# Operand splits and the last gate rank placed later in the queues, and the down projection's summed products accumulated in one PSUM bank

## The chip, the cores and the metric

The kernel runs on one core of a Trainium2 chip. The metric is device time in microseconds (us), the median of the runs of one program. The engines are PE (TensorE), DVE (VectorE), ACT (ScalarE), POOL (GpSimd) and SP (SyncE, which here only issues DMAs).

## What is computed

One hybrid decoder layer on a 1024 x 1024 activation in float32: two attention groups, an output projection, and a gated feed-forward part with a causal convolution of width 3. Only the feed-forward part is touched by the change:

```python
h = rmsnorm(x, ffn_norm_g[l])
u = causal_dwconv(h @ w_up[l], conv_w[l], conv_b[l])
gate, val = jnp.split(u, 2, axis=-1)
x = x + (jax.nn.silu(gate) * val) @ w_down[l]
```

`w_up` is 1024 x 5632 (2816 gate and 2816 value columns), `w_down` is 2816 x 1024.

## The kernel before

**Precision.** Each float32 factor is split into a high part (a cast on ACT) and a low part (source minus high part, on DVE or POOL). `mm3` makes one product block from three matmuls: high x high, high x low, low x high. A **split** below is the cast and the subtraction; lines 762 and 763 split an activation operand, lines 908 and 910 a weight.

**Seven products instead of eight.** The feed-forward matrices are multiplied as 2 x 2 blocks with seven products by the scheme of Strassen and Winograd. `PORD` names them: a11, s2, a22, a12, s1, s3, s4. Each has an activation operand (`bmat`: b11, t2, t4, b21, t1, t3, b22 in that order) and a weight block (raw, or one of four sums that POOL makes on lines 881 to 890). One product is 4 x 3 matmuls of 128 x 512, or 3 x 3 in the last two chunks.

**Steps.** There are 34 steps of seven products. Steps 0 to 21 are the up projection; each leaves one rank of 128 gate and 128 value rows, which DVE combines, convolves (`conv`, line 1007, four long instructions a rank), and gates (line 1083 on ACT, line 1084 on DVE). Steps 22 to 33 are the down projection in three chunks `c` of the inner dimension (`KN` = 4, 3, 3 block pairs), four steps each. The last two ranks (20 and 21) go through a plain product at the end.

**Where one operand set gives way to the next.** Activation operands wait in DRAM (`td`). In the last step of the up projection, and in the last step of a chunk, each product is followed by `operands(n, ...)`: SP loads that product's next operand blocks into seven buffers `st`, ACT and DVE split them (the first block of each is split on POOL) into the tiles that PE has just read for the last time. There are three such handovers: step 21 to 22, 25 to 26 and 29 to 30.

**The y tiles.** In the down projection DVE adds each product from its PSUM bank into the output tiles `y` in SBUF. These tiles take the memory of the up projection's pool `upp`, which holds the convolution's tiles, so their first load (line 1102) can only run when the last of those is done with. Each product has a bank of its own; eight banks go round.

**What sets the order.** SP's instructions keep the order in which the program is written. For the other engines a list scheduler decides by priority, which is the place in the program unless `tc.high_priority(offset=...)` shifts it; each engine then runs its own list strictly in order. Weights are made at most four products ahead (`ahead_to(idx + 4)`) into three pair buffers `wspl`. Weight splits of step 22 stand on POOL and DVE, later ones all on DVE.

Of the kernel before, what the change touches and what calls it, by code (L numbers as in the profile page):

```python
# [9 lines left out]
F32 = mybir.dt.float32  # L10
F32R = mybir.dt.float32r
BF16 = mybir.dt.bfloat16
AF = mybir.ActivationFunctionType
ALU = mybir.AluOpType
# [3 lines left out]
P = 128  # L18
# [7 lines left out]
NJ = DFF // P  # L26
NPRE = 3
# [19 lines left out]


PORD = ("a11", "s2", "a22", "a12", "s1", "s3", "s4")
LO_UP = ("s3", "s1")  # L50
LO_FIRST = ("a11", "a22", "a12")

ORDER, ORDER_LAST = (0, 1, 3, 2), (0, 1, 3, 2)
LAG, LEAD, RATE, PAUSE, TRC = 3, 40.0, 1.327, 12.0, 0.67
UA = 3

PARTS = ((0, 512), (512, 256), (768, 256))
NORM_AT = ((1, 3), (2, 3), (3, 0))
# [10 lines left out]
def layer(ctx, tc, xT, wqk, wv0, wv, wout, wup, wdn, cols, fbias, yT):  # L69
    nc = tc.nc  # L70
    act = nc.scalar.activation
# [84 lines left out]
                    if d == 1:  # L156
                        n.split(min(n.pieces, int(frac * n.pieces + 0.01)))

    def mm3(ps, ah, al, bh, bl, start, stop):
        nc.tensor.matmul(ps, ah, bh, start=start, stop=False)  # L160
        nc.tensor.matmul(ps, ah, bl, start=False, stop=False)  # L161
        nc.tensor.matmul(ps, al, bh, start=False, stop=stop)  # L162

    small = ctx.enter_context(tc.tile_pool(name="small", bufs=4))

# [168 lines left out]
    with tc.tile_pool(name="ps_0", bufs=6, space=PSUM) as ps0, \  # L334
# [31 lines left out]
        for k in range(KT):  # L366
# [4 lines left out]
            for u in range(2):  # L371
                wh, wl = w_qk[u].get()
                for c in range(2):
                    if k == 0:
                        psq[u, c] = ps0.tile([P, 512], F32, name="p0")
                    sl = slice(c * 512, (c + 1) * 512)
# [363 lines left out]
    def bank():  # L740
        turn[0] += 1
        if (turn[0] - 1) % 8 < 6:
            return ps_u.tile([P, 512], F32, name="u")
        return ps_p.tile([P, 512], F32, name="pj")
# [27 lines left out]
    for c in range(2):  # L772
        sl = slice(c * 512, (c + 1) * 512)
        for m in range(KT):
# [8 lines left out]
            if c == 0 and m < 2:  # L783
                ps = box[m]
            else:
                ps = bank()
                for k in range(4):
                    w, _ = out_step(1 + c, m, c, k, ps)
# [27 lines left out]
    tp_ = ctx.enter_context(tc.tile_pool(name="tblk", bufs=1, side="right"))  # L816
    t2, t4, t1, t3, b22 = (halves(tp_, n) for n in ("t2", "t4", "t1", "t3", "b22"))

    def product(w, o, b, n=4):
        ps = bank()  # L820
        wh, wl = w
        for k in range(n):
            sl = slice(o + k * P, o + (k + 1) * P)
            mm3(ps, wh[:, sl], wl[:, sl], b[k][0], b[k][1], k == 0, k == n - 1)
        return ps

    steps = [("u", j, 4) for j in range(NJ)] + [(c, mp, KN[c]) for c in range(NCH) for mp in range(KT // 2)]
    NS = len(steps)
# [17 lines left out]
    first(1)  # L846
    first(2)

    stream = [(j, n) for j in range(NS) for n in PORD if j >= NPRE or n not in ("a11", "a12")]
    made, tiles, plain = {}, {}, {}  # L850
    pos = [0]

# [150 lines left out]
    def conv(t, u, us):  # L1003
        cw = C_CW + 3 * u
        act(t, us, AF.Identity, scale=col[:, cw + 2:cw + 3], bias=gcol(C_CB, u))
        for s, tap in ((1, 1), (2, 0)):
            nc.vector.scalar_tensor_tensor(t[:, s:], us[:, :T - s], col[:, cw + tap:cw + tap + 1],  # L1007
                                           t[:, s:], op0=ALU.mult, op1=ALU.add)
# [5 lines left out]
    def operand(dst, src, eng=None):  # L1014
        raw = stp.tile([P, 512], F32, name="st")
        nc.sync.dma_start(raw, src)
        split(dst, raw, eng)

    def operands(n, c):
        for i in range(KN[c]):  # L1020
# [24 lines left out]
    for j in range(NJ):  # L1045
# [31 lines left out]
            if j == NJ - 1:  # L1077
                operands(n, 0)
        tv = upp.tile([P, T], F32, name="tv")
        conv(tv, 2 * j + 1, ub)  # L1080
        tg = stg.tile([P, T], F32, name="tg", tag="hl")
        conv(tg, 2 * j, ua[j])
        act(tg, tg, AF.Silu)
        tt(tg, tg, tv, ALU.mult)
        if j % 2 == 0:
            prev = tg
        elif j < PLAIN:
# [23 lines left out]
    for s in range(NJ, NS):  # L1111
        c, mp, kn = steps[s]
        ev, od_ = 2 * mp, 2 * mp + 1
        for n in PORD:
            ahead_to(idx + 4)
            if s == NS - 1 and n == PORD[3]:
                plain_split(0)
            if s == NS - 1 and n == PORD[-1]:
                plain_split(1)
            w, o = made[s, n]  # L1120
            idx += 1
            ps = product(w, o, bmat[n], kn)
            if c == 0 and n == PORD[0]:
                if mp == 0:
                    load_y(0)
                elif mp < KT // 2 - 1:
                    load_y(mp + 1)
            if c == 0 and mp == 0 and n == PORD[3]:
                load_y(1)
            if n == "a11":  # L1130
                m1s = fin.tile([P, 512], F32, name="m1s")
                nc.scalar.copy(m1s, ps)
                tt(y[ev, 0], y[ev, 0], m1s, ALU.add)
            elif n == "s2":
                u2 = fin.tile([P, 512], F32, name="u2")
                tt(u2, ps, m1s, ALU.add)
                tt(y[ev, 1], y[ev, 1], u2, ALU.add)
            elif n == "a22":
                tt(y[od_, 0], y[od_, 0], ps, ALU.subtract)
            elif n == "a12":  # L1140
                tt(y[ev, 0], ps, y[ev, 0], ALU.add)
            elif n == "s1":
                tt(y[od_, 1], ps, y[od_, 1], ALU.add)
                tt(y[ev, 1], ps, y[ev, 1], ALU.add)
            elif n == "s3":
                tt(u2, ps, u2, ALU.add)
                tt(y[od_, 1], y[od_, 1], u2, ALU.add)
                tt(y[od_, 0], y[od_, 0], u2, ALU.add)
            elif n == "s4":
                tt(y[ev, 1], ps, y[ev, 1], ALU.add)  # L1150
            if mp == KT // 2 - 1 and c < NCH - 1:
                operands(n, c + 1)
            if c == 1 and mp == 1 and kind[n] < 4:
                i = kind[n]
                rest[i // 2, i % 2] = spare[i]
                operand(spare[i], td[-1][i])
# [124 lines left out]
```

## Time and profile before

| | us |
|---|---|
| median of 3 runs (lowest to highest) | 1423.91 (1421.47 to 1424.47) |
| the profiled execution | 1431.94 |
| its span, first to last instruction | 1430.2 |
| PE busy in the span | 1310.7 (92%) |
| DVE busy | 1111.7 (78%) |
| POOL busy | 773.8 (54%) |
| ACT busy | 620.7 (43%) |

The profiled execution is 8.0 us longer than the median. Times inside the trace count from the start of its span. The up projection's last step runs from about 1148 to 1168, the down projection from there to 1391, and the plain product and the final norm fill the rest. Busy PE time is modelled; counts of matmuls in a stretch, and the gaps between their starts, are the surer reading.

### The profile page before, as it was taken

To read this page: it belongs to the slowest core of one execution; us is meant where nothing else is said; L and a number is where in the kernel's file an instruction comes from. 1 tells how busy PE (TensorE), PEld (TensorE's weight loads), DVE (VectorE), ACT (ScalarE), POOL (GpSimd) and SP (SyncE) were. 2 spreads that over 40 slices of the span, in tenths; PEclk is the share of its full clock that TensorE was granted. 3 is DMA by queue.
4 is the path that set the end of the run, shared out by engine and by line. 5 is a ranking of instruction groups with operands and counts; after the bars stand their busy time and mean duration, and the time that the engine had idled before them with its cause. 6 is when DMAs were issued, how large, how long until landed. Compare 5 with 4: busy or idle time off the path is not lost.

```text
span 1430.2 us, 19128 instructions
## 1 busy us (share of the span) xinstructions
PE 1310.7 (92%) x6640; PEld 1075.8 (75%) x6640; DVE 1111.7 (78%) x1638; ACT 620.7 (43%) x1128; POOL 773.8 (54%) x680
## 2 busy tenths in 40 slices
PE   7999999999898886789989999999999989999895
PEld 5878878887687765678766788888888867878684
DVE  6246655655677677787889999988888899899987
ACT  5134434444554455354454433443433453444334
POOL 7343454445657583540004788778787774554423
PEclk9999999999999999899979999999999999999997
DMA  5555455644544455546521222333322365444303
GB/s 180 182 161 175 131 154 159 189 135 119 161 112 141 118 143 143 170 128 221 205 81 67 91 98 106 111 111 111 110 96 96 96 219 206 163 147 152 114 30 118
DMA packets 97232, 194.88 MB, mean 136 GB/s; under 512 B 8681, under 2 KB 35689, under 8 KB 97137
## 3 DMA queue, kind: packets, MB, share of 16 engines
q1 hardware_dynamic: 96272, 193.04, 42.9%
q8 instruction: 52, 0.85, 0.3%
q10 hardware_dynamic: 864, 0.64, 0.1%
q14 instruction: 44, 0.35, 0.1%
HBM read 132.79 MB, written 60.85 MB: 135 GB/s over the span
## 4 chain that ended last, share of the span: by engine, by line
PE 49%; DVE 18%; DMA 17%; POOL 6%; issue 5%; ACT 2%; SPq 2%; DVEq 0%; POOLq 0%; ACTq 0%
PE u L161 7%; PE u L162 7%; PE u L160 7%; PE pj L160 5%; PE pj L162 5%; PE pj L161 5%; DMA q<-qkd 4%; DVE fbt L494 3%; DMA vd<-vs 3%; DMA st<-td 2%; PE tp L506 2%; PE o L527 2%; DVE wl L910 2%; DMA wraw<-in_wv_dram 2%; PE o L526 1%
## 5 line engine op out<-in xcount | busy, mean ns | idle before, releaser
L881 POOL TENSOR_TENSOR s<-wraw 128x512 f32<-128x512 f32 (+1 forms) x32 | 52.7, 1647 | 213.9 <-DMA wraw<-in_wup_dram 141.3
L495 POOL TENSOR_TENSOR w<-w,fbt 128x128 f32<-128x128 f32 (+3 forms) x64 | 91.2, 1434 | 90.9 <-DVE fbt L494 59.8
L908 ACT CAST wh<-s 128x512 fp32r<-128x512 f32 (+1 forms) x136 | 79.5, 591 | 122.4 <-POOL s L882 69.8
L494 DVE TENSOR_TENSOR_SCAN fbt<-fbt 128x128 f32<-128x128 f32 (+3 forms) x64 | 102.9, 1616 | 27.9 <-ACT fbt L481 24.2
L142 POOL TENSOR_SCALAR wh<-wraw 128x256 fp32r<-128x256 f32 (+1 forms) x112 | 55.4, 511 | 111.7 <-DMA wraw<-in_wqk_dram 58.8
L506 PE MATMUL tp<-ident,w 128*128 128x128 f32 x576 | 93.2, 280 | 24.1 <-DVE pl L515 10.7
L160 PE MATMUL pj<-xh,wh 128*128 128x512 f32 x224 | 102.1, 456 | 3.7 <-DVE yf L294 3.7
L506 PEld LDWEIGHTS tp<-ident,w 128*128 128x128 f32 x576 | 70.2, 143 | 43.2 <-DVE pl L515 14.3
L910 POOL TENSOR_TENSOR wl<-wraw,wh 128x512 fp32r<-128x512 f32 x58 | 100.0, 1730 | 0.0
L515 DVE TENSOR_TENSOR pl<-tp,ph 128x512 fp32r<-128x512 f32 x96 | 64.9, 685 | 40.1 <-ACT ph L514 39.7
L162 PE MATMUL pj<-xh,wl 128*128 128x512 f32 x224 | 90.6, 404 | 0.0
L161 PE MATMUL pj<-xl,wh 128*128 128x512 f32 x224 | 90.3, 403 | 0.0
L486 ACT ACTIVATE w<-w,m 128x128 f32<-128x128 f32 (+3 forms) x64 | 49.7, 776 | 92.0 <-DVE m L476 86.9
L144 POOL TENSOR_TENSOR wl<-wraw,wh 128x256 fp32r<-128x256 f32 (+1 forms) x112 | 89.1, 814 | 0.3
L1007 DVE SCALAR_TENSOR_TENSOR tg<-ua,col,tg 128x1023 f32<-128x1023 f32 (+1 forms) x44 | 89.1, 2026 | 0.0
L908 ACT CAST wh<-wraw 128x512 fp32r<-128x512 f32 (+1 forms) x96 | 55.2, 590 | 70.0 <-DMA wraw<-in_wdn_dram 27.4
L481 ACT ACTIVATE fbt<-s 128x512 f32<-128x512 f32 (+2 forms) x96 | 47.6, 496 | 86.7 <-PE s L471 40.2
L490 POOL TENSOR_SCALAR w<-w,l 128x128 f32<-128x128 f32 (+3 forms) x64 | 48.0, 755 | 61.5 <-DVE l L489 31.0
L278 PE MATMUL pj<-wh,xh 128*128 128x256 f32 (+1 forms) x256 | 78.5, 307 | 0.8 <-DVE yf L294 0.8
L514 ACT CAST ph<-tp 128x512 fp32r<-128x512 f32 x96 | 55.6, 589 | 53.9 <-PE o L526 34.1
L910 POOL TENSOR_TENSOR wl<-s,wh 128x512 fp32r<-128x512 f32 x44 | 73.4, 1668 | 9.4 <-ACT wh L908 9.2
L467 PE MATMUL s<-kh,q 128*128 128x256 f32 (+2 forms) x192 | 69.5, 364 | 8.4 <-DMA kh<-qkd 6.4
(366 smaller groups left out, 4520.0 us busy)
## 6 DMA issues: line engine op xcount, KB each, us to landing
wraw<-in_wup_dram SPq DMA_DIRECT2D x47, 512.0 KB, 3.7
st<-td SPq DMA_DIRECT2D x74, 256.0 KB, 4.1
qkd<-hl SPq DMA_DIRECT2D x32, 512.0 KB, 3.2
td<-tg SPq DMA_DIRECT2D x44, 256.0 KB, 2.3
vd<-vs SPq DMA_DIRECT2D x32, 256.0 KB, 4.6
q<-qkd SPq DMA_DIRECT2D x16, 512.0 KB
kh<-qkd SPq DMA_DIRECT2D x32, 256.0 KB, 16.5
kl<-qkd SPq DMA_DIRECT2D x32, 256.0 KB, 17.3
```

Source lines behind the costliest of these rows:

```text
L144: eng.tensor_tensor(self.lo[:, sl], self.raw[:, sl], f32(self.hi[:, sl]), ALU.subtract)
L160: nc.tensor.matmul(ps, ah, bh, start=start, stop=False)
L161: nc.tensor.matmul(ps, ah, bl, start=False, stop=False)
L162: nc.tensor.matmul(ps, al, bh, start=False, stop=stop)
L278: nc.tensor.matmul(ps[:, :n], xh[k][:, sl], h, start=(k == 0), stop=False)
L467: nc.tensor.matmul(s[:, :cn], qb, kh[:, c0:c0 + cn], start=True, stop=False)
L494: nc.vector.tensor_tensor_scan(qt[:, rev], qt[:, rev], qt[:, rev], 1.0, ALU.mult, ALU.bypass)
L495: nc.gpsimd.tensor_tensor(w[:, :n], w[:, :n], qt[:, T - n + 1:T + 1], ALU.mult)
L506: nc.tensor.transpose(tp[:, a * 256 + b * P:a * 256 + (b + 1) * P], ws[2 * g + b][:, kb * P:(kb + 1) * P], ident)
L908: nc.scalar.copy(h[:, o:o + w], src)
L910: eng.tensor_tensor(l[:, o:o + w], src, f32(h[:, o:o + w]), ALU.subtract)
L1007: nc.vector.scalar_tensor_tensor(t[:, s:], us[:, :T - s], col[:, cw + tap:cw + tap + 1], t[:, s:], op0=ALU.mult, op1=ALU.add)
```

## The change

It does three things. First, the split inside `operand` gets a priority 70 places later than where it is written, and the convolution and gate of the last rank (j = 21) 210 places later. Second, the down projection runs its products in another order, `PORD_D`: a11, a22, s1, s2, a12, s4, s3; weights are made in that order too. Third, s2 is accumulated onto the bank that holds a11, s3 onto that same bank afterwards, and s4 onto the bank of s1 (`ONTO`), so that the sums a11 + s2, a11 + s2 + s3 and s1 + s4 stand in PSUM. The intermediate tiles `m1s` and `u2` go, with the ACT copy and three DVE additions of a step: eight additions remain of eleven, each reading a bank.

```diff
+PORD_D = ("a11", "a22", "s1", "s2", "a12", "s4", "s3")
+ONTO = {"s2": "a11", "s4": "s1", "s3": "a11"}
+YIELD = 70
...
-    def product(w, o, b, n=4):
-        ps = bank()
+    def product(w, o, b, n=4, onto=None):
+        ps = onto or bank()
...
-            mm3(ps, wh[:, sl], wl[:, sl], b[k][0], b[k][1], k == 0, k == n - 1)
+            mm3(ps, wh[:, sl], wl[:, sl], b[k][0], b[k][1], k == 0 and onto is None, k == n - 1,
+                onto is not None)
...
-    stream = [(j, n) for j in range(NS) for n in PORD if j >= NPRE or n not in ("a11", "a12")]
+    stream = [(j, n) for j in range(NS) for n in (PORD if j < NJ else PORD_D)
+              if j >= NPRE or n not in ("a11", "a12")]
...
-        split(dst, raw, eng)
+        with tc.high_priority(offset=-YIELD):
+            split(dst, raw, eng)
...
-        conv(tv, 2 * j + 1, ub)
         tg = stg.tile([P, T], F32, name="tg", tag="hl")
-        conv(tg, 2 * j, ua[j])
-        act(tg, tg, AF.Silu)
-        tt(tg, tg, tv, ALU.mult)
+        with tc.high_priority(offset=0 if j < NJ - 1 else -3 * YIELD):
+            conv(tv, 2 * j + 1, ub)
+            conv(tg, 2 * j, ua[j])
+            act(tg, tg, AF.Silu)
+            tt(tg, tg, tv, ALU.mult)
...
-        for n in PORD:
+        on = {}
+        for n in PORD_D:
...
-            ps = product(w, o, bmat[n], kn)
+            ps = on[n] = product(w, o, bmat[n], kn, on.get(ONTO.get(n)))
...
-            if n == "a11":
-                m1s = fin.tile([P, 512], F32, name="m1s")
-                nc.scalar.copy(m1s, ps)
-                tt(y[ev, 0], y[ev, 0], m1s, ALU.add)
-            elif n == "s2":
-                u2 = fin.tile([P, 512], F32, name="u2")
-                tt(u2, ps, m1s, ALU.add)
-                tt(y[ev, 1], y[ev, 1], u2, ALU.add)
+            if n in ("a11", "a12"):
+                tt(y[ev, 0], ps, y[ev, 0], ALU.add)
             elif n == "a22":
                 tt(y[od_, 0], y[od_, 0], ps, ALU.subtract)
-            elif n == "a12":
-                tt(y[ev, 0], ps, y[ev, 0], ALU.add)
-            elif n == "s1":
+            elif n in ("s2", "s4"):
+                tt(y[ev, 1], ps, y[ev, 1], ALU.add)
+            else:
                 tt(y[od_, 1], ps, y[od_, 1], ALU.add)
-                tt(y[ev, 1], ps, y[ev, 1], ALU.add)
-            elif n == "s3":
-                tt(u2, ps, u2, ALU.add)
-                tt(y[od_, 1], y[od_, 1], u2, ALU.add)
-                tt(y[od_, 0], y[od_, 0], u2, ALU.add)
-            elif n == "s4":
-                tt(y[ev, 1], ps, y[ev, 1], ALU.add)
+                if n == "s3":
+                    tt(y[od_, 0], ps, y[od_, 0], ALU.add)
```

**PE at the first down step.** Each row is the first matmul of a product; its eleven followers are left out. The number behind `u` or `pj` is the bank's tile, the name after the arrow is the operand. Before, steps 22 and 23 begin so:

```order
L160 MATMUL u_11306<-b11h0_7179,wh_11123 128x512
...
L160 MATMUL u_11328<-t2h0_7627,wh_11123 128x512
...
L160 MATMUL pj_11348<-t4h0_7635,wh_11198 128x512
...
L160 MATMUL pj_11364<-b21h0_7187,wh_11198 128x512
...
L160 MATMUL u_11397<-t1h0_7643,wh_11302 128x512
...
L160 MATMUL u_11414<-t3h0_7651,wh_11302 128x512
...
L160 MATMUL u_11438<-b22h0_7659,wh_11344 128x512
...
L160 MATMUL u_11454<-b11h0_7179,wh_11344 128x512
```

Now the same eight products stand so:

```order
L165 MATMUL u_11306<-b11h0_7179,wh_11123 128x512
...
L165 MATMUL u_11326<-t4h0_7635,wh_11123 128x512
...
L165 MATMUL pj_11344<-t1h0_7643,wh_11191 128x512
...
L165 MATMUL pj_11385<-b21h0_7187,wh_11298 128x512
...
L165 MATMUL u_11445<-b11h0_7179,wh_11340 128x512
...
L165 MATMUL u_11306<-t2h0_7627,wh_11191 128x512
...
L165 MATMUL pj_11344<-b22h0_7659,wh_11298 128x512
...
L165 MATMUL u_11306<-t3h0_7651,wh_11340 128x512
```

The sixth, seventh and eighth write banks that hold an earlier product (u_11306, pj_11344, u_11306); the scheduler has put step 23's a11 ahead of them, as the fifth.

**DVE at the end of the up projection.** The rows run from the last convolution of rank 21 (`tg`, with 1023 columns) to the first additions into `y`. Before:

```order
L1007 SCALAR_TENSOR_TENSOR tg_11276<-ua_11140,col_76,tg_11276 128x1023
L910 TENSOR_TENSOR wl_11345<-wraw_11240,wh_11344 128x512
L1007 SCALAR_TENSOR_TENSOR tg_11276<-ua_11140,col_76,tg_11276 128x1022
L763 TENSOR_TENSOR b22l1_7662<-st_11260,b22h1_7661 128x512
L763 TENSOR_TENSOR b22l2_7664<-st_11264,b22h2_7663 128x512
L1084 TENSOR_TENSOR tg_11276<-tg_11276,tv_11272 128x1024
L763 TENSOR_TENSOR b22l3_7666<-st_11268,b22h3_7665 128x512
L910 TENSOR_TENSOR wl_11387<-s2_11389,wh_11386 128x512
L1136 TENSOR_TENSOR u2_11341<-u_11328,m1s_11323 128x512
L910 TENSOR_TENSOR wl_11387<-wraw_11238,wh_11386 128x512
L1133 TENSOR_TENSOR y0_0_11286<-y0_0_11286,m1s_11323 128x512
```

Now:

```order
L768 TENSOR_TENSOR b22l3_7666<-st_11264,b22h3_7665 128x512
L1014 SCALAR_TENSOR_TENSOR tg_11269<-ua_11140,col_76,tg_11269 128x1023
L1014 SCALAR_TENSOR_TENSOR tg_11269<-ua_11140,col_76,tg_11269 128x1022
L917 TENSOR_TENSOR wl_11341<-wraw_11304,wh_11340 128x512
L1093 TENSOR_TENSOR tg_11269<-tg_11269,tv_11268 128x1024
L1141 TENSOR_TENSOR y0_0_11282<-u_11306,y0_0_11282 128x512
L1141 TENSOR_TENSOR y0_0_11282<-pj_11385,y0_0_11282 128x512
L1143 TENSOR_TENSOR y1_0_11284<-y1_0_11284,u_11326 128x512
L1147 TENSOR_TENSOR y1_1_11285<-pj_11344,y1_1_11285 128x512
L1141 TENSOR_TENSOR y2_0_11286<-u_11445,y2_0_11286 128x512
L1145 TENSOR_TENSOR y0_1_11283<-u_11306,y0_1_11283 128x512
```

All of b22's splits now stand ahead of the last gate multiplication (line 1093, 1084 before), and the addition that reads a11's bank u_11306 stands right behind it. Between rank 20's last convolution and that multiplication DVE has 38 instructions before and 39 now, the same set with one b22 split more.

**DVE at the handover from step 29 to 30.** From the last step's s2 addition, before (there the order is s3, then s4):

```order
L1146 TENSOR_TENSOR u2_12360<-u_12464,u2_12360 128x512
L910 TENSOR_TENSOR wl_12461<-wraw_12306,wh_12460 128x384
L1147 TENSOR_TENSOR y7_1_11301<-y7_1_11301,u2_12360 128x512
L1148 TENSOR_TENSOR y7_0_11300<-y7_0_11300,u2_12360 128x512
L763 TENSOR_TENSOR t3l1_7654<-st_12481,t3h1_7653 128x512
L763 TENSOR_TENSOR t3l2_7656<-st_12485,t3h2_7655 128x512
L1150 TENSOR_TENSOR y6_1_11299<-u_12495,y6_1_11299 128x512
L910 TENSOR_TENSOR wl_12519<-s1_12427,wh_12518 128x384
L1133 TENSOR_TENSOR y0_0_11286<-y0_0_11286,m1s_12532 128x512
```

Now, from the s4 addition to the first addition of step 30:

```order
L1145 TENSOR_TENSOR y6_1_11295<-u_12310,y6_1_11295 128x512
L768 TENSOR_TENSOR t2l1_7630<-st_12351,t2h1_7629 128x512
L768 TENSOR_TENSOR t2l2_7632<-st_12355,t2h2_7631 128x512
L1147 TENSOR_TENSOR y7_1_11297<-u_12258,y7_1_11297 128x512
L1149 TENSOR_TENSOR y7_0_11296<-u_12258,y7_0_11296 128x512
L917 TENSOR_TENSOR wl_12443<-wraw_12256,wh_12442 128x384
L917 TENSOR_TENSOR wl_12443<-s2_12387,wh_12442 128x384
L1141 TENSOR_TENSOR y0_0_11282<-u_12450,y0_0_11282 128x512
```

Fewer additions stand there; step 30's addition of a11, which its s2 product waits for, still has two operand and two weight splits within the seven rows ahead of it.

## Rows read from the trace of the kernel before

**Rows 1.** Busy time by stretch: window, length, engines' busy us (instructions), granted clock, DMA.

```profile
core 0: us, PE busy (x) PEld busy (x) DVE busy (x) ACT busy (x) POOL busy (x), PEclk, DMA share, GB/s
1155.90:1199.10 43.20, 35.26 (x134) 27.47 (x133) 41.83 (x40) 25.85 (x44) 30.39 (x18) 0.88 0.53 174
1240.00:1275.00 35.00, 33.05 (x141) 26.23 (x141) 31.17 (x41) 18.89 (x36) 20.73 (x14) 1.00 0.55 187
1306.00:1340.00 34.00, 29.06 (x122) 22.35 (x121) 32.24 (x41) 17.87 (x34) 19.29 (x14) 1.00 0.60 196
1340.00:1391.00 51.00, 51.00 (x221) 41.38 (x220) 42.78 (x69) 15.23 (x30) 14.99 (x12) 1.00 0.17 52
```

**Rows 2.** Waits of PE, 1150 to 1400: releaser, total us, times, longest.

```profile
PE u L162 <- DVE wl L910: 8.2, 4, 4.9
PE pj L162 <- DVE wl L910: 5.1, 3, 3.0
PE pj L161 <- POOL b22l L763: 1.6, 1, 1.6
PE u L161 <- DVE b22l L763: 0.2, 1, 0.2
```

**Rows 3.** Timeline of PE: start, duration, instruction, idle time before it and releaser.

```profile
1173.58 0.79 PE L162 MATMUL u<-b11h,wl 128*128 128x512 f32 x1 [4.92 <-DVE wl L910]
...
1178.44 0.41 PE L161 MATMUL u<-t2l,wh 128*128 128x512 f32 x1
...
1187.44 0.50 PE L162 MATMUL pj<-b21h,wl 128*128 128x512 f32 x1 [3.02 <-DVE wl L910]
...
1200.29 0.40 PE L160 MATMUL u<-b11h,wh 128*128 128x512 f32 x1
...
1203.09 0.40 PE L160 MATMUL u<-t2h,wh 128*128 128x512 f32 x1
```

**Rows 4.** Timeline of DVE at the first handover.

```profile
1154.65 1.27 DVE L1007 SCALAR_TENSOR_TENSOR tg<-ua,col,tg 128x1022 f32<-128x1022 f32 x1
...
1167.81 5.12 DVE L763 TENSOR_TENSOR t4l<-st,t4h 128x512 fp32r<-128x512 f32 x3
...
1174.05 1.28 DVE L763 TENSOR_TENSOR b21l<-st,b21h 128x512 fp32r<-128x512 f32 x2
...
1197.85 1.21 DVE L1084 TENSOR_TENSOR tg<-tg,tv 128x1024 f32<-128x1024 f32 x1
1198.99 0.68 DVE L763 TENSOR_TENSOR b22l<-st,b22h 128x512 fp32r<-128x512 f32 x1
...
1202.12 0.68 DVE L1133 TENSOR_TENSOR y<-y,m1s 128x512 f32<-128x512 f32 x1
```

**Rows 5.** Timeline of POOL beside it.

```profile
1165.60 1.74 POOL L763 TENSOR_TENSOR t4l<-st,t4h 128x512 fp32r<-128x512 f32 x1
...
1170.76 1.62 POOL L763 TENSOR_TENSOR b21l<-st,b21h 128x512 fp32r<-128x512 f32 x1
1174.83 1.65 POOL L763 TENSOR_TENSOR t1l<-st,t1h 128x512 fp32r<-128x512 f32 x1 [2.45 <-ACT t1h L762]
```

**Rows 6.** Timeline of SP: start, issue time, transfers.

```profile
1199.12 3.64 SPq L1102 DMA_DIRECT2D y<-x2f  x8
```

**Rows 7.** DMA issues, 1199.0 to 1199.5: size, median us to landing.

```profile
y<-x2f SPq DMA_DIRECT2D x2, 256.0 KB, 2.6
```

**Rows 8.** DVE groups by form, 1200 to 1391: count, busy us, mean ns, idle before.

```profile
L1137 DVE TENSOR_TENSOR y<-y,u 128x512 f32<-128x512 f32 x12 | 13.2, 1103 | 0.1
L1133 DVE TENSOR_TENSOR y<-y,m1s 128x512 f32<-128x512 f32 x12 | 10.6, 881 | 2.8 <-ACT m1s L1132 2.8
...
L1136 DVE TENSOR_TENSOR u<-u,m1s 128x512 f32<-128x512 f32 x10 | 6.8, 679 | 0.1
...
L1146 DVE TENSOR_TENSOR u<-u,u 128x512 f32<-128x512 f32 x8 | 5.4, 680 | 0.0
...
L1144 DVE TENSOR_TENSOR y<-u,y 128x512 f32<-128x512 f32 x8 | 5.4, 678 | 0.0
```

More of the change, by code (lines that the diff above doesn't have):

```diff
@@ L157, in ahead, with mm3 @@
                         n.split(min(n.pieces, int(frac * n.pieces + 0.01)))
[L159 to L162, printed above, removed]
+    def mm3(ps, ah, al, bh, bl, start, stop, more=False):
+        nc.tensor.matmul(ps, ah, bh, start=start, stop=False, skip_group_check=more)
+        nc.tensor.matmul(ps, ah, bl, start=False, stop=False, skip_group_check=more)
+        nc.tensor.matmul(ps, al, bh, start=False, stop=stop, skip_group_check=more)
     small = ctx.enter_context(tc.tile_pool(name="small", bufs=4))
@@ L1113, in layer @@
         ev, od_ = 2 * mp, 2 * mp + 1
-        for n in PORD:
+        on = {}
+        for n in PORD_D:
             ahead_to(idx + 4)
-            if s == NS - 1 and n == PORD[3]:
+            if s == NS - 1 and n == PORD_D[3]:
                 plain_split(0)
-            if s == NS - 1 and n == PORD[-1]:
+            if s == NS - 1 and n == PORD_D[-1]:
                 plain_split(1)
@@ L1121, in layer @@
             idx += 1
-            ps = product(w, o, bmat[n], kn)
-            if c == 0 and n == PORD[0]:
+            ps = on[n] = product(w, o, bmat[n], kn, on.get(ONTO.get(n)))
+            if c == 0 and n == PORD_D[0]:
                 if mp == 0:
@@ L1127, in layer @@
                     load_y(mp + 1)
-            if c == 0 and mp == 0 and n == PORD[3]:
+            if c == 0 and mp == 0 and n == PORD_D[3]:
                 load_y(1)
-            if n == "a11":
-                m1s = fin.tile([P, 512], F32, name="m1s")
-                nc.scalar.copy(m1s, ps)
-                tt(y[ev, 0], y[ev, 0], m1s, ALU.add)
-            elif n == "s2":
-                u2 = fin.tile([P, 512], F32, name="u2")
-                tt(u2, ps, m1s, ALU.add)
-                tt(y[ev, 1], y[ev, 1], u2, ALU.add)
+            if n in ("a11", "a12"):
+                tt(y[ev, 0], ps, y[ev, 0], ALU.add)
             elif n == "a22":
                 tt(y[od_, 0], y[od_, 0], ps, ALU.subtract)
-            elif n == "a12":
-                tt(y[ev, 0], ps, y[ev, 0], ALU.add)
-            elif n == "s1":
+            elif n in ("s2", "s4"):
+                tt(y[ev, 1], ps, y[ev, 1], ALU.add)
+            else:
                 tt(y[od_, 1], ps, y[od_, 1], ALU.add)
-                tt(y[ev, 1], ps, y[ev, 1], ALU.add)
-            elif n == "s3":
-                tt(u2, ps, u2, ALU.add)
-                tt(y[od_, 1], y[od_, 1], u2, ALU.add)
-                tt(y[od_, 0], y[od_, 0], u2, ALU.add)
-            elif n == "s4":
-                tt(y[ev, 1], ps, y[ev, 1], ALU.add)
+                if n == "s3":
+                    tt(y[od_, 0], ps, y[od_, 0], ALU.add)
             if mp == KT // 2 - 1 and c < NCH - 1:
```

## The prediction

> **What bounds the kernel now.** I read the stretches first, then the waits of PE, then the timelines of the engines it waits for. In the stretch 1340 to 1391 nothing stops PE: 221 matmuls start in 51.00 us, one every 0.231 us [rows 1]. That is the yardstick: a product of twelve matmuls takes 2.77 us, one of nine 2.08 us. Counted against it, three stretches of the down projection fall short [rows 1]: at the first handover 134 matmuls in 43.2 us, so 43.2 - 134 x 0.231 = 12.3 us are lost; at the second 35.0 - 141 x 0.231 = 2.5 us; at the third 34.0 - 122 x 0.231 = 5.8 us. The waits say by whom: nearly all are for the low part of a weight or an operand on DVE [rows 2]. DVE is busy for 41.83 of 43.2, 31.17 of 35 and 32.24 of 34 us there [rows 1]. So PE bounds the feed-forward part except at the handovers, where DVE's list is too long. All stalls together, 12.3 + 2.5 + 5.8 = 20.6 us, are the most that a better order can give back. Nothing ahead of about 1156 changes: both programs have the same lists there.
>
> **Handover 1, the new chain.** Before, no product of step 22 needs DVE to have added anything: each has its own bank, and the eight banks let PE run on while the last gate is still in DVE's list. The eight products of step 22 and of step 23's a11 are done when the next product starts, at 1203.1 [rows 3].
>
> Now the sixth product goes onto a11's bank, so PE may start it only after DVE has added a11 into y. That addition needs y loaded; the load needs the memory of the convolution tiles, which is free after the last gate multiplication. The old trace shows this link: the multiplication ends at 1197.85 + 1.21 = 1199.06 [rows 4], and SP issues the first y load at 1199.12 [rows 6]. It cost nothing then, since only DVE's additions waited. So the question is when that multiplication ends now.
>
> Between rank 20's last convolution, which ends at 1154.65 + 1.27 = 1155.9 [rows 4], and that multiplication, DVE has the same 38 instructions as before and one b22 split more (0.68 us without POOL beside it [rows 4]). It was busy for 41.83 of those 43.2 us [rows 1], so nothing can be squeezed out by order alone: the end moves to about 1199.7. Then 2.6 us from issue to landing [rows 7], 0.68 us for the addition (the price of one that reads a bank [rows 8]) and some 0.1 us of signalling: the sixth product starts at 1203.1. Three products of 2.77 us follow; the eighth ends at 1211.4 instead of 1203.1, **8.3 us later**. All stalls of the old order lie before that point and are swallowed, not added: the first five products have 35 us for 14 us of work. One slow start is added. After its 4.92 us wait PE took 4.86 us for the next eleven starts (1173.58 to 1178.44 [rows 3]), 0.44 us each, which is the 1.2 GHz level against the 2.4 GHz of 0.231 us: 4.86 - 11 x 0.231 = 2.3 us lost. Part of that now falls into the fifth product, whose own low weight stands just ahead of the gate multiplication and which is covered by the wait for y; I take 1.7 of the 2.3 us.
>
> Together **+10 us**. Low end: a split costs between 5.12 / 3 = 1.71 us, when POOL works beside it, and 1.28 / 2 = 0.64 us, when it does not [rows 4, 5]; three splits that escape POOL would bring the multiplication 3.2 us forward, and with a smaller clock loss the term is +5. High end: the b11 splits stand behind two weights and a gate multiplication now, so their buffers, and the seven-buffer chain of loads behind them, come free later; 3 us of waiting on DVE and the full clock loss make it +14.
>
> **Handovers 2 and 3, less work on DVE.** A step loses three additions of 0.68 us (lines 1136, 1144, 1146), and the additions of lines 1133 and 1137, which read SBUF twice at 0.88 and 1.10 us, become reads of a bank at 0.68 us [rows 8]: 3 x 0.68 + 0.20 + 0.42 = 2.66 us a step, 32 us over twelve steps. Only what lies ahead of a stall counts. The splits of a handover lie over two steps, so up to 5.3 us of DVE work goes from in front of the last stall. The 2.5 us of handover 2 could go wholly, and of the 5.8 us of handover 3 some 5.3 us: 7.8 us at most. Something is late next: step 30's s2 product waits for the addition of a11, which has four splits within the seven rows ahead of it, and the products between them give 2 x 2.08 = 4.2 us of cover. In the old trace a split among POOL's takes up to 1.7 us [rows 4], so four of them can use up 4 to 7 us. I let 1 to 2 us come back at each of the two: **-5 us**, between -7.8 and -3.
>
> **What costs nothing.** In the other steps, too, s2, s4 and s3 wait for an addition, with two products (4.2 or 5.5 us) of cover in front of each. DVE was busy for 42.78 of 51 us in 1340 to 1391 [rows 1]; 2.66 us less in 14.5 us leaves it idle a third of the time, so an addition of 0.68 us gets through. 0, at most +3 (0.25 us a step). ACT loses twelve copies, but was busy for only 15.23 of 51 us [rows 1]: 0. On SP, step 23's weight loads are queued behind b22's last four loads; the weights split from them stand behind all of b22's splits on DVE anyway, which cover that: 0; if the cover were gone it would show as DVE waiting, which the +14 contains.
>
> **Sum**, on the profiled execution: +10 - 5 + 0 = +5 us, 1431.9 to 1436.9 us. That execution lies 8.0 us above the median of the runs shown; I carry the difference over unchanged: 1423.9 + 5 = **1428.9 us**. About 0.2%, 2.8 us, is what can be told from no change.
>
> **Rival 1, faster: the splits get cheaper.** The first term hangs on when DVE reaches the gate multiplication. Beside POOL three t4 splits took 5.12 us; two b21 splits took 1.28 us while POOL waited, from 1172.4 to 1174.8 [rows 4, 5]. If the new order has POOL waiting for operands while DVE splits, seven or eight of the slow splits fall from 1.71 to 0.64 us (7.5 x 1.07 = 8 us), and the multiplication ends some 8 us earlier, at 1191 to 1192. The eighth product then ends when it did before, and only the -5 us remain: 1419 us. It decides for faster from about 1192.4 on (7.3 us earlier), where the sum passes -2.8. Against it: POOL has as many instructions in that stretch as before, and where it waits, it mostly waits for a buffer that DVE frees. In the Trainium skill, SBUF — State Buffer, Who interferes with whom, a VectorE instruction with two SBUF inputs and a GpSimd instruction that reads SBUF shut each other out, whichever comes second; by that rule the slow splits go with POOL's place in time alone, which is this rival, and the rows named agree (1.71 against 0.64 us).
>
> **Rival 2, no difference:** both terms a little off the middle, +6.5 and -6.5. 1424 us.
>
> **Rival 3, much slower: every step waits for its banks.** DVE's list is strict; an addition that stands behind a split whose source is late holds PE at s2, s4 or s3 in every step. At 2 us a step, the eleven steps after the first add 22 us to the 5: 1451 us. For it: additions do stand behind pairs of weight splits. Against it: DVE's third of idle time, above. PSUM — Partial Sum Buffer of the Trainium skill, PSUM bank collisions raise a hardware error, says that a matmul and a VectorE read of one bank must be kept apart by semaphores, which speaks against summing in a bank that is being read; by it the wait cannot be dropped. No run here shows a collision.
>
> **How the numbers follow.** My forecast, slower by 2.8 to 14 us through the chain at handover 1, gets 0.58; its own range is 1427 to 1438. Rival 1 gets 0.15, rival 2 0.22, rival 3 0.05. Slower is 0.58 + 0.05 = 0.63. Low bound: +5 - 7.8 = -2.8 us, 1421. High bound: +14 - 3 + 2 = +13 us, 1437. That leaves out most of rivals 1 and 3 and the ends of the forecast, about 0.2.
>
> **What would show it.** In the new trace: PE waiting at the first matmul of s2 in step 22, released by a DVE addition into y, near 1203; a y load issued within 0.1 us of the last gate multiplication, and that near 1199.7. At handovers 2 and 3 PE's lost time should be 1 to 5 us together instead of 8.3, with a part of it released by additions instead of splits. Wrong would be: a gate multiplication before 1193 (rival 1), no wait at all at s2, or waits for additions in every step (rival 3).

## The result: 0.9% slower, about 13 us, not 5

The changed kernel took 1438.7 us (1435.74 to 1441.05) beside 1424.19 us (1421.47 to 1425.84) for the one before: a ratio of 1.0093, interval 1.007 to 1.0116. The direction was as forecast. The size was not: 1438.7 us lies above the stated range of 1421 to 1437 us, and the 13 us of the ratio (14.5 between the medians) are more than twice the forecast 5.

The profiled execution of the changed kernel has a span of 1439.3 us. It reached step 21 at 1142.8 us, the one before at 1148.3, so 5.5 us have to be added to its times where they are compared with rows of before. Stretches of busy time (window, length, busy us and instructions of PE, PEld, DVE, ACT, POOL, granted clock, DMA), first the first handover (the window of [rows 1], 5.5 us earlier), then step 26, steps 27 and 28, the third handover, and the rest of the down projection:

```profile
1150.40:1193.60 43.20, 28.69 (x105) 21.02 (x104) 42.07 (x40) 24.96 (x41) 28.53 (x18) 0.82 0.52 172
...
1262.00:1285.60 23.60, 19.97 (x75) 15.79 (x74) 20.13 (x27) 8.60 (x17) 10.54 (x9) 0.86 0.38 120
1285.60:1315.00 29.40, 29.40 (x128) 23.84 (x127) 21.34 (x35) 9.10 (x18) 9.19 (x9) 1.00 0.28 90
1315.00:1349.00 34.00, 30.11 (x128) 23.32 (x127) 30.73 (x44) 18.29 (x35) 18.98 (x14) 1.00 0.63 201
1349.00:1392.90 43.90, 43.90 (x190) 35.62 (x189) 28.92 (x45) 9.94 (x20) 12.80 (x11) 1.00 0.18 58
```

At the first handover PE started 105 matmuls where it had started 134 [rows 1], at 0.82 of the full clock instead of 0.88. Step 26, which had a clock of 1.00 in its stretch before, now has 0.86. The last stretch shows that the change did what it says: PE is never held there, and DVE is busy for 28.92 of 43.9 us, two thirds, where 84% were needed before [rows 1].

The waits of PE from 1150 to 1400 us (total, times, longest), which answer to [rows 2]:

```profile
PE u L165 <- DVE y L1141: 5.3, 3, 3.6
PE u L167 <- DVE wl L917: 5.2, 1, 5.2
PE u L165 <- ACT wh L915: 2.9, 1, 2.9
PE pj L166 <- POOL t1l L768: 2.6, 1, 2.6
PE u L165 <- DVE y L1145: 2.6, 2, 1.6
PE pj L166 <- DVE t1l L768: 2.4, 1, 2.4
```

The waits for `y` are new: 5.3 + 2.6 us, in steps 22, 26, 29 and 30 alone. Waits for a low weight, which were 13.3 us, are down to one of 5.2.

From the starts of the products on PE the program can be cut into five stretches: H1 from the first product of step 21 to that of step 24, then steps 24 and 25, H2 for steps 26 to 28, H3 from step 29 to the first plain product (at 1384.5 in the kernel before), and the tail. The us of each, for before, after and those experiments that take the change apart:

| | H1 | 24, 25 | H2 | H3 | tail | ratio to before |
|---|---|---|---|---|---|---|
| before | 71.5 | 39.0 | 46.4 | 79.2 | 45.7 | 1 |
| after | 82.2 | 39.3 | 50.6 | 78.1 | 46.4 | 1.0093 |
| order and shared banks (e1) | 83.6 | 39.8 | 50.2 | 81.7 | 47.5 | 1.0125 |
| later places alone (e2) | 72.1 | 39.0 | 48.0 | 81.0 | 45.4 | 1.0032 |
| order alone (e3) | 74.9 | 39.0 | 46.1 | 83.9 | 46.2 | 1.0052 |
| order and later places (e7) | 71.9 | 40.0 | 46.5 | 87.2 | 46.4 | 1.0052 |

Each row is one execution. For a whole kernel such a profile stands 0.7 to 3.4 us off the median, and the one of before 8.0 (it reached step 21 later than any other run); so the ratios carry the verdict, and the stretches say where. Below, a ratio is also given in us of 1424.

### The profile page after: what moved, and what is told of

It reads as the page before. It is cut to its first block, busy times and chain, and to the rows that moved or that the text cites. A ratio compares the mean times of both kernels' runs of the same rounds, so it can differ in the third digit from the quotient of the medians.

```text
span 1439.3 us, 19089 instructions
## 1 busy us (share of the span) xinstructions
PE 1313.8 (91%) x6640; PEld 1076.8 (75%) x6640; DVE 1089.9 (76%) x1602; ACT 615.7 (43%) x1116; POOL 764.0 (53%) x680
## 4 chain that ended last, share of the span: by engine, by line
PE 49%; DMA 20%; DVE 15%; POOL 6%; issue 5%; ACT 3%; SPq 3%; DVEq 0%; POOLq 0%; ACTq 0%
PE u L166 9%; PE u L167 9%; PE u L165 9%; DMA q<-qkd 5%; PE pj L165 4%; PE pj L167 4%; PE pj L166 4%; DMA vd<-vs 3%; DVE fbt L499 2%; DMA wraw<-in_wqk_dram 2%; DMA st<-td 2%; PE tp L511 2%; DMA kl<-qkd 2%; PE o L532 1%; DMA fbt<-nfd 1%
## 5 line engine op out<-in xcount | busy, mean ns | idle before, releaser
L888 POOL TENSOR_TENSOR s<-wraw 128x512 f32<-128x512 f32 (+1 forms) x32 | 46.9, 1465 | 200.1 <-DMA wraw<-in_wup_dram 144.9
L147 POOL TENSOR_SCALAR wh<-wraw 128x256 fp32r<-128x256 f32 (+1 forms) x112 | 51.3, 475 | 112.5 <-DMA wraw<-in_wqk_dram 59.6
L149 POOL TENSOR_TENSOR wl<-wraw,wh 128x256 fp32r<-128x256 f32 (+1 forms) x112 | 93.0, 849 | 0.3
```

What stands on the lines that cost most here:

```text
L149: eng.tensor_tensor(self.lo[:, sl], self.raw[:, sl], f32(self.hi[:, sl]), ALU.subtract)
```

## The experiments

**Which part of the change costs.** Four kernels leave parts out. The first, e1, has no part of the shift in priority:

```diff
-YIELD = 70
+YIELD = 0
```

> The change without its first part: operand splits and the last gate rank keep their places, the new product order and the shared banks stay. Theory (the loss at the first handover is the chain last gate multiplication, y load, addition of a11, s2 product, which only the shared bank creates; the loss at the second is the a11 addition standing behind the operand splits): the chain is whole, so the time stays near the changed kernel's 1438.7 us, between 1434 and 1441. Rival L (it is the later splits and the later gate rank that hold PE): back near 1424 us, 1421 to 1428. Rival W (it is the other order of the products and weights): 1434 to 1441, like the theory.

Measured: 1.0125 (1.01 to 1.0149), +18 us, just above the theory's range and far from rival L. The later places are no cause of the loss here; with the shared banks they save 4.6 us.

The second, e2, has that part alone (old order in `PORD_D`, `ps = bank()` for each product, the old additions).

> Only the first part of the change: splits 70 and the last gate rank 210 places later, with the old product order, a bank for each product, and the old additions. Theory (shared banks): no s2 product waits for an addition, so about 1424 us, 1420 to 1428. Rival L (the later places cost): 1434 us or more. Rival W (the order of the products costs): about 1424 us.

Measured: 1.0032 (1.0011 to 1.0052), +4.6 us. Not nothing, as the theory had it, and not rival L's 10 us. PE now waits for operands where it had waited for weights (12.1 us in all against 2.2).

The third, e3, has the new order alone, with a bank for each product.

> Only the second part: products and weights in the new order a11, a22, s1, s2, a12, s4, s3, each with a bank of its own, old additions, nothing later. Theory (shared banks): 1421 to 1428 us, since nothing on PE waits for an addition. Rival L: about 1424 us too. Rival W (the order costs, since weights and operands come ready in another order than PE takes them): 1434 us or more.

Measured: 1.0052 (1.0035 to 1.0068), +7.4 us, between the two. The order by itself costs more than half of what the whole change costs: 3.4 us in H1 and 4.7 in H3. Its waits, 1150 to 1400 us:

```profile
PE u L167 <- DVE wl L917: 18.1, 8, 6.5
PE pj L167 <- DVE wl L917: 2.1, 3, 1.0
PE pj L165 <- DVE ub L1079: 0.5, 1, 0.5
```

It is the same kind of wait as in the kernel before [rows 2], 20.2 us instead of 13.3.

The fourth, e4, gives the first step of each chunk banks of its own:

```diff
+        sep = s in (22, 26, 30)
...
-            ps = on[n] = product(w, o, bmat[n], kn, on.get(ONTO.get(n)))
+            ps = on[n] = product(w, o, bmat[n], kn, None if sep else on.get(ONTO.get(n)))
```

> The changed kernel, but in the first step of each chunk (22, 26, 30) every product has a bank of its own and the old additions; the other nine steps share banks. Theory: these three steps are where the shared bank meets DVE's full list, so the 10.7 us of the first handover and the 3.6 us wait with the slow clock behind it at the second go: 1438.7 - 10.7 - 4 = 1424 us, 1420 to 1428. Rivals L and W: no more than a third of the loss comes back, 1434 us or more. If 1428 to 1434, the nine other steps cost too.

Measured: 1.0056 (1.0034 to 1.0077), +8 us. H1 falls from 82.2 to 72.6 us, so the shared bank in step 22 is what H1 lost by. The time lies in the third range, where the nine other steps cost too. H2 stays at 50.6: the wait for an addition has moved from step 26 to step 27 (2.8 us at 1279.28). H3 grows from 78.1 to 81.9 us, so in step 30 banks of its own are no gain.

**Order and later places together.** e7 is the changed kernel with a bank for each product in all steps; it closes the table above.

> The changed kernel with a bank for each product and the old additions in all twelve steps: the new order and the later places alone. If the parts just add up, the two alone (+4.5 and +7.4 us) give 1424 + 12 = 1436, 1433 to 1439, and the shared banks cost only 2 to 3 us. If the later places mend what the new order breaks, as they did with the shared banks (4.6 us less), 1427, 1424 to 1431, and the shared banks cost 10 us or more.

Measured: 1.0052 (1.0038 to 1.0066), +7.4 us, between both outcomes. Set against the changed kernel it gives the price of the shared banks: 1.0093 / 1.0052 is 0.4%, **5.8 us**. The other **7.4 us** are the order and the later places. The price of one part hangs on the others: without the later places the shared banks cost 1.0125 / 1.0052, 10.4 us (e1 beside e3). By the intervals, each of these two prices is uncertain by about 4 us. In the profiles they stand almost wholly in H3, 87.2 us against 79.2. Its waits:

```profile
PE u L166 <- DVE t4l L768: 3.0, 2, 2.3
PE pj L166 <- DVE t2l L768: 3.0, 1, 3.0
PE pj L166 <- POOL t1l L768: 2.9, 1, 2.9
PE u L167 <- DVE wl L917: 2.4, 3, 1.1
```

**The chain at the first handover.** e5 gives the y tiles of a11 and s1 of step 22 memory of their own:

```diff
+        if j == NJ - 1:
+            for m in range(2):
+                y[m, m] = yown.tile([P, 512], F32, name=f"y{m}_{m}")
+                nc.sync.dma_start(y[m, m], x2f[m][m])
...
```

> The changed kernel, but the two y tiles that the a11 and the s1 product of step 22 are added into have memory of their own and are loaded before step 21, so their loads don't need the convolution's memory; nine products now stand on PE ahead of the one that needs a y loaded behind the last gate multiplication. Theory (chain gate multiplication, y load, addition, s2): the stretch from step 21 to the ninth product of the down projection, 54.8 us before and 65.4 us after, returns to 54 to 57 us, and the time falls by about 10 us to 1429, 1425 to 1432. Rival (PE is held there by weights and operands that come late from DVE in the new order, whatever y does): the stretch stays above 61 us, the time above 1434.

Measured: 1.0071 (1.0052 to 1.009), +10 us; the time is a miss, 3.1 us less than the changed kernel instead of 10. The ninth product starts 56.3 us after step 21 does, as expected, but then s3 of step 22 waits 1.8 us for the next y, PE is slow after that, and H1 comes to 76.6 us, 5.6 less than 82.2.

e6 lets ACT copy the banks, so that PE waits for a copy:

```diff
+            src = ps
+            if n in ("a11", "s1", "s2"):
+                src = cpp.tile([P, 512], F32, name="cp")
+                nc.scalar.copy(src, ps)
...
```

> The changed kernel, but ACT copies the banks of a11, s1 and a11 + s2 to two SBUF tiles with memory of their own, and DVE adds from the copies: the next product onto such a bank waits for ACT's copy and not for DVE's list (three ACT copies a step more, DVE adds as many). Theory (the shared banks cost because PE waits for DVE's list, at the first handover through y, at the second and third for the a11 and s2 additions, and each such wait is followed by a slow clock): the first stretch returns to 54 to 57 us as with y's own memory, the additions' waits (8.1 us in all in the changed kernel) go, and the time is 1420 to 1428. Rival (ACT's list is as late as DVE's, since its casts wait for loads): above 1432.

Measured: 1.0058 (1.0039 to 1.0077), +8.3 us or 1432.4 on the scale of 1424.2: at the lower end of the rival's range, and 5.0 us less than the changed kernel. The first stretch, from step 21 to the ninth product, came down from 65.4 to 56.6 us, as the theory had it. But the waits for the shared banks did not go, 8.5 us in all beside 8.1; they have a new name, not a new size:

```profile
PE u L165 <- ACT cp L1144: 5.2, 5, 1.9
PE pj L165 <- ACT cp L1144: 3.3, 2, 1.7
```

ACT's timeline in step 26 shows what the copy of s1 stands behind:

```profile
1268.00 0.51 ACT L915 CAST wh<-wraw 128x384 fp32r<-128x384 f32 x1 [4.78 <-DMA wraw<-in_wdn_dram]
1268.42 0.58 ACT L1144 COPY cp<-pj 128x512 f32<-128x512 f32 x1
```

ACT was idle for 4.78 us, in front of a cast whose weight was still being loaded, while the copy that PE waited for (1.72 us, at 1269.05) was next in its list. ACT, busy for 13.13 of the 25 us from 1250 on, was no quicker to answer than DVE, since its list is strict too.

**POOL beside DVE.** e8 leaves out POOL's subtractions at H2 and H3.

```diff
-            split(dst, raw, eng)
+            if eng is None or idx <= 22 * 7:
+                split(dst, raw, eng)
+            else:
+                nc.scalar.copy(dst[0], raw)
```

> The changed kernel, but at the second and third handover POOL doesn't make the low part of the first block of an operand (14 subtractions left out, so that block keeps an old low part). DVE has the same list. Theory P (the additions come late because DVE's splits take up to twice as long beside POOL's): the wait for the a11 addition in step 26, 3.6 us, shrinks below 1.5 us, the stretch from step 26 to 29 falls from 50.6 to 45 to 48 us, and the time to 1431 to 1435. Theory Q (DVE's list is too long there, with or without POOL's splits): the wait stays above 2.5 us, the time 1436 to 1441.

Measured: 1.0027 (1.0013 to 1.0042), +3.9 us, 9.4 less than the changed kernel, better than theory P asked. From 1200 us on PE waits for nothing up to the plain product, for no `y` either: H2 44.3 and H3 73.2 us. DVE's groups from 1235 to 1345 us (count, busy us, mean ns, idle before) show why. The changed kernel:

```profile
L768 DVE TENSOR_TENSOR t4l<-st,t4h 128x512 fp32r<-128x512 f32 x5 | 6.1, 1226 | 0.0
L768 DVE TENSOR_TENSOR t2l<-st,t2h 128x512 fp32r<-128x512 f32 x5 | 5.7, 1167 | 0.0
L768 DVE TENSOR_TENSOR t3l<-st,t3h 128x512 fp32r<-128x512 f32 x4 | 4.3, 1085 | 0.0
L1141 DVE TENSOR_TENSOR y<-u,y 128x512 f32<-128x512 f32 x9 | 6.2, 683 | 2.9 <-PE u L167 2.9
```

Without POOL's subtractions:

```profile
L768 DVE TENSOR_TENSOR t4l<-st,t4h 128x512 fp32r<-128x512 f32 x5 | 3.4, 685 | 1.0 <-ACT t4h L767 1.0
L768 DVE TENSOR_TENSOR t2l<-st,t2h 128x512 fp32r<-128x512 f32 x5 | 3.5, 728 | 0.0
L768 DVE TENSOR_TENSOR t3l<-st,t3h 128x512 fp32r<-128x512 f32 x4 | 2.7, 683 | 0.6 <-ACT t3h L767 0.6
```

In these three groups the same split takes 1.1 to 1.2 us beside POOL's subtractions and 0.68 to 0.73 without them; two of the other four groups took 0.68 us beside them as well. The 32 operand splits of DVE in this stretch take 31.9 us and 23.3 us in all. An addition that reads a bank takes 0.68 us either way.

e9 makes use of that on the kernel before; DVE takes the 14 subtractions over:

```diff
-                    nc.gpsimd if i == 0 else None)
+                    nc.gpsimd if i == 0 and c == 0 else None)
```

> The kernel before, with one edit: at the second and third handover DVE makes the low part of an operand's first block too, not POOL (14 subtractions move). Theory P (what makes DVE late there is POOL's subtractions beside it, not the length of DVE's list): DVE gets 14 x 0.68 = 9.5 us more, but its splits fall from about 1.0 to 0.7 us, and the stalls of the old kernel, 2.5 and 6 us, mostly go: 1416 to 1422 us against 1424. Theory Q (the length of the list): 2 to 5 us slower, 1426 to 1430.

Measured: **0.9948** (0.9935 to 0.9961), 7.4 us faster: theory P, and the best version of this study, ahead of both kernels. DVE makes 14 splits more at these handovers, but needs no more time for them: 46 operand splits take 32.3 us between 1235 and 1345 us, where 32 took 32.3. One of the seven groups, before and now:

```profile
L763 DVE TENSOR_TENSOR t2l<-st,t2h 128x512 fp32r<-128x512 f32 x5 | 7.6, 1542 | 0.0
...
L763 DVE TENSOR_TENSOR t2l<-st,t2h 128x512 fp32r<-128x512 f32 x7 | 4.6, 695 | 0.0
```

And PE waits less:

```profile
1250.00:1268.00 18.00, 18.00 (x79) 14.64 (x78) 18.00 (x31) 7.99 (x15) 6.59 (x5) 1.00 0.34 116
1298.00:1333.00 35.00, 32.50 (x137) 25.12 (x137) 33.23 (x54) 20.43 (x40) 10.61 (x8) 1.00 0.57 190
```

In the first of these stretches, the second handover, PE starts 79 matmuls in 18 us, one every 0.228: nothing is lost there, although DVE is busy all the time. H2 is 44.0 and H3 76.7 us, 2.4 and 2.5 less than before; the profiles place 4.9 of the 7.4 us there.

At the third handover PE's waits for low weights from DVE fall from 4.95 us in four to 1.31 in two. At the second the cause is less clear. In the kernel before, PE's longest wait there was for a low part that POOL itself made, and such parts no longer exist in e9:

```profile
1274.03 0.50 PE L161 MATMUL pj<-b22l,wh 128*128 128x512 f32 x1 [1.60 <-POOL b22l L763]
```

Whether DVE's shorter splits or the end of that wait gave the 2.4 us there was not separated.

e10 (`None` for all three handovers) adds the first one.

> The kernel before, with all operand splits on DVE at all three handovers (21 subtractions move). Theory P: as the run with two handovers, and the first one gains or stays: 1412 to 1422 us. Theory Q: 5 us slower or more. Since DVE is busy for 41.8 of 43.2 us at the first handover and POOL has weight splits there as well, the first handover may lose 2 to 4 us even if P holds for the others.

Measured: 0.9956 (0.9941 to 0.9971), 6.3 us faster, no better than with two. H1 is 72.5 us instead of 71.5, so at the first handover nothing is gained.

e11 and e12 make the edit of e9 in the changed kernel and in e5.

> The changed kernel, with the 14 subtractions on DVE at the second and third handover: the complete computation, where the earlier run left them out and lost the 9.4 us. Theory P: most of those 9.4 us stay gained, 1428 to 1433 against 1438.7. Theory Q: 1438 or more.

> The changed kernel with both: two y tiles in memory of their own, and the 14 subtractions on DVE at the second and third handover. If the two losses stand apart in time and add up, -3.2 (own y as measured) and -6 to -9: 1426 to 1430, a few us above the kernel before, since the first handover still waits for weights and operands.

Measured: 1.0056 (1.0036 to 1.0076) and 1.004 (1.0023 to 1.0056), 1432.2 and 1429.9 us on the scale of 1424.2: both in their ranges. The gain of 5.3 us for e11 is less than the 9.4 of e8, where the 14 subtractions were not made at all: from 1200 us on PE waits again, 2.0 us for `y` and 3.7 us for operands and weights, where in e8 it waited for nothing.

**What the order and the later places cost.** e13 makes the edit of e9 in e7.

> The new order and the later places with a bank for each product (1.0052 of the kernel before, 7.4 us), and the 14 subtractions moved from POOL to DVE at the second and third handover. If what the order and the later places lose there (about 8 us by the profiles) is DVE held up by POOL, it goes: 0.994 to 1.000 of the kernel before. If it is weights and operands that are loaded later in the new order, whatever POOL does: 1.002 or more.

Measured: 1.0021 (1.0006 to 1.0037), at the edge of the second range. Beside e9 it is clear: 1.0021 / 0.9948 is 0.7%, 10 us, for the order and the later places where POOL is out of the way, and 7.4 us where it isn't. So POOL is a loss of its own and not the reason for theirs. It does change where theirs stands: against e9 the profile of e13 is 3.8 us longer in H2 and 3.7 in H3, where e7 had 8.0 in H3 and next to nothing in H2.

e14 puts a12 fourth in the order alone, so that the next weights are loaded earlier:

```diff
-PORD_D = ("a11", "a22", "s1", "s2", "a12", "s4", "s3")
+PORD_D = ("a11", "a22", "s1", "a12", "s2", "s4", "s3")
```

> The new order alone (1.0052), but with a12 fourth, a11, a22, s1, a12, s2, s4, s3. A step's next weights are loaded when a12's are made; with a12 fifth, SP has those two loads behind all loads of the last operand, with a12 fourth ahead of the last operand's three, as in the kernel before. Theory W (these late loads are what the new order costs): 0.999 to 1.002 of the kernel before, and PE's wait of 3.8 us for a raw weight's low part in step 30 goes. Rival (the order in which DVE's splits and PE's products meet, whatever the loads): 1.004 or more.

Measured: 1.0094 (1.006 to 1.0127), in the rival's range and slower than e3. Theory W falls: the two loads are issued 4.9 us after the start of step 30 instead of 10.6, and PE's wait of 3.8 us in that step goes, but H3 is 83.5 us beside 83.9 in e3, and H1 and H2 are 2.0 and 3.8 us longer. The waits now are for operands and weights alike:

```profile
PE pj L167 <- DVE wl L917: 5.2, 3, 3.2
PE u L167 <- DVE wl L917: 4.9, 3, 2.2
PE u L166 <- POOL b22l L768: 1.9, 1, 1.9
```

e15 makes both edits in the changed kernel.

> The changed kernel with both mends: a12 fourth, and the 14 subtractions on DVE at handovers two and three. At the first handover seven products now stand on PE ahead of the first that needs a y, not five, so 2 x 2.77 us of the 10 us come back; at the others the additions come earlier: 0.999 to 1.004 of the kernel before, against 1.0093. Above 1.006 the theory of the chain or that of POOL would be missing something.

Measured: 1.0042 (1.0027 to 1.0056), +6 us, at the upper end: H1 76.7 us, the 5.5 that two more products of cover should bring, and H2 and H3 together 122.2 instead of 128.7.

e16 adds one shared bank to e9, in the old order:

```diff
-            ps = product(w, o, bmat[n], kn)
+            ps = product(w, o, bmat[n], kn, on if n == "s4" and s > NJ else None)
...
```

> The kernel before with the 14 subtractions on DVE at handovers two and three (0.9948), and one shared bank: s4 goes onto s1's bank in the old order, from step 23 on, so that a step has one addition less, with s3's 2.1 to 2.8 us as cover. Theory: DVE's list is still the bound at the third handover, so 0.992 to 0.995. If the wait for s1's addition meets DVE's list there: 0.996 to 1.000.

Measured: 1.0016 (1.0 to 1.0032), 9.7 us slower than e9 (1.0016 / 0.9948) and above both ranges. One addition less a step, and PE waits for the one that is left, first in step 23:

```profile
1209.13 0.47 PE L160 MATMUL pj<-b22h,wh 128*128 128x512 f32 x1 [2.62 <-DVE y L1144]
```

DVE had reached that addition late because two weight splits (1.27 and 1.55 us, with 1.94 us of idle time before them) stood ahead of it in its list. By the profiles of e9 and e16, 4.1 us of the loss stand in H1 and 3.0 between step 24 and the plain product; 3.8 us more stand in the tail, where no bank is shared, and are not explained.

## Where the prediction was right and where it failed

**The chain at the first handover: right.** The timelines of the changed kernel, DVE, SP and PE:

```profile
1193.34 1.23 DVE L1093 TENSOR_TENSOR tg<-tg,tv 128x1024 f32<-128x1024 f32 x1 [0.58 <-ACT tg L1092]
1197.23 0.69 DVE L1141 TENSOR_TENSOR y<-u,y 128x512 f32<-128x512 f32 x1 [2.66 <-DMA y<-x2f]
```

```profile
1194.59 3.65 SPq L1111 DMA_DIRECT2D y<-x2f  x8
```

```profile
1192.81 0.80 PE L167 MATMUL u<-b11h,wl 128*128 128x512 f32 x1 [5.18 <-DVE wl L917]
...
1197.97 0.80 PE L165 MATMUL u<-t2h,wh 128*128 128x512 f32 x1 [0.52 <-DVE y L1141]
```

With the 5.5 us added, the multiplication ends at 1200.1 (forecast 1199.7), the y load is issued within 0.02 us of it, and s2 starts at 1203.5 (forecast 1203.1). H1 is 10.7 us longer; the term was +10. One thing was the other way round. The prediction had the wait of the fifth product, step 23's a11, for its low weight covered by the wait for `y`. In fact the a11 product waited 5.18 us for that weight, a neighbour of the gate multiplication in DVE's list, and the wait for `y` behind it is 0.52 us only. Both ends of that list arrive together, so taking the y load away (e5) gave back half, by letting the scheduler put two more products ahead of that weight; banks apart (e4, e7) gave back 9.6 and 10.3 of the 10.7 us.

**The step that failed: the -5 us for handovers 2 and 3.** H2 and H3 together went from 125.6 to 128.7 us: 3.1 more where 5 less were forecast, 4.2 more in H2 and 1.1 less in H3. PE's lost time in their two stretches is 23.6 - 75 x 0.231 = 6.3 and 34 - 128 x 0.231 = 4.4 us, 10.7 together, where the prediction expected 1 to 5. Two things were wrong in that term.

The first is the size of what comes back at the second handover, which I had put at 1 to 2 us. There the addition of a11 came 7 us after its product, behind the splits of b22 and t3, two additions of step 25 and a weight, and the wait was paid twice:

```profile
1270.37 0.40 PE L167 MATMUL pj<-t1h,wl 128*128 128x512 f32 x1
1274.40 0.77 PE L165 MATMUL u<-t2h,wh 128*128 128x512 f32 x1 [3.63 <-DVE y L1141]
...
1280.48 0.40 PE L167 MATMUL pj<-b21h,wl 128*128 128x512 f32 x1
```

From 1274.40 to 1280.48 there are 14 starts, 0.43 us each, at a granted clock of 0.50, the 1.2 GHz level; at 0.231 us they take 3.2. So 3.63 us of waiting cost 2.8 more in clock, and 6.4 us came back. The 2.5 us lost there before did go (1.6 of them had been a wait for POOL's b22l [rows 2], not for DVE's list), which leaves about the 4.2 us measured. The forecast counted the clock for one wait of the first handover and for none here.

The second is the order and the later places, costed at nothing. The working for handovers 2 and 3 consists of additions saved and of waits for additions. That DVE makes operands and weights there in another order, and PE wants them in another order, has no term, although the first handover had shown what a split at the wrong place costs. e7 measures it: +7.4 us, and +8 us in H3 by the profiles.

Between e7 and the changed kernel H2 grows by 4.1 us and H3 shrinks by 9.1, together -5.0, the very figure of the forecast. That is luck: 9.1 is more than the 5.8 us that the kernel before lost at the third handover at all, and it is saved from an H3 that the new order had first made longer. In the same way 5.8 us from the shared banks, beside +5 in the forecast's sum, and 7.4 from a term that wasn't there are the 13.2; taken apart from the other side, the order costs 7.4, the shared banks 10.4, and the later places give 4.6 back.

Why the new order is worse is only partly settled. Earlier weight loads gained nothing (e14), and the loss stays when POOL's subtractions go (e13). The waits are mostly for low parts on DVE, of weights in e3 and of operands in e7; that DVE's list stands in an order that fits PE's less well is the likely reason, but which pairs of rows do it was not tried.

A slip in the sum changes nothing: the high bound counts +2 us for the other steps, where the working allows +3. With +3 it would be 1438 us, still below the measured time.

**What cost nothing: right.** Steps 24 and 25 took 39.3 us instead of 39.0, and steps 27 and 28 and those from step 31 on ran without a wait, so rival 3 is out. **Rival 1** is out too: the gate multiplication ended at 1200.1, not before 1193. Its mechanism, cheaper splits, does exist at handovers 2 and 3, as e8 and e9 show: it has to be forced by moving POOL's work, and then that move is worth 7.4 us to the kernel before. At the first handover, where rival 1 had placed it, e10 gained nothing. The Trainium skill says (SBUF — State Buffer, Who interferes with whom) that a VectorE instruction with at most one SBUF input, outside its two-port modes, doesn't contend with GpSimd. The traces agree: additions that read a bank kept 0.68 us beside POOL, splits, which read SBUF twice, mostly did not.

The Trainium skill has a rule that bears on the change and that the prediction left out: independent groups of matmuls should rotate through different banks, so that emptying one overlaps with the next (Perfetto Trace Analysis, Matmuls). Summed products are not independent groups in the strict sense, but here each bank is read between two of them, and this case agrees: the shared banks cost 5.8 us in the changed kernel, and e16, with one a step, is 9.7 us slower than e9.

## What to carry to other kernels

Letting products share a bank saves additions on VectorE, but it puts that engine's strict list into TensorE's path: find, for each product that goes onto a used bank, what stands ahead of the addition that frees it, and count the slow clock behind such a wait too (2.8 us behind 3.63 here). When order or priorities change too, each needs a term of its own at every place where an engine's list is full. And before taking instructions off a full VectorE, look at what GpSimd does beside it: 14 subtractions moved from GpSimd to VectorE made the kernel before 7.4 us faster.

## Not expected of the hardware

- A split of 128 x 512 on VectorE takes 0.68 us alone and, in the slower groups, 1.1 to 1.5 us on average while GpSimd makes subtractions beside it; the GpSimd subtraction itself takes 1.3 to 1.8 us. With 14 of them moved to VectorE, its 46 splits took the same 32.3 us as 32 before, and the kernel was 7.4 us faster.
- After 3.63 us of waiting TensorE ran 14 matmuls at the 1.2 GHz level (granted clock 0.50), 2.8 us more than at 2.4 GHz.
